# A two-layer decoder trunk on one core: the first stage's loads, products and factors reordered, and the last store moved

## The chip, the cores and the metric

The kernel runs on one core of a Trainium2 chip. Its engines each take their own list of instructions in order: TensorE (PE, with weight loads shown apart as PEld), VectorE (DVE), ScalarE (ACT), GpSimd (POOL) and SyncE (SP), which here only issues transfers. Sixteen DMA engines move the data. The metric is the device time of one execution in microseconds (us).

## The reference, cut to what matters

The input x is a matrix of 1024 rows (positions) by 1024 columns in float32. Two layers follow; each has a token mixer and a SwiGLU feed-forward network, each behind an RMS norm and added to the running sum h.

```python
def rms_norm(x, g):
    y = x * rsqrt(mean(x * x, axis=-1, keepdims=True) + 1e-6)
    return y * g

h = x
# layer 0: RG-LRU block
hn = rms_norm(h, mix_norm[0])
u = hn @ lru_w_in + lru_b_in                 # 1024 x 2048: [gate branch | recurrent branch]
rec = causal_depthwise_conv(u[:, 1024:], conv_w, conv_b)
# block-diagonal gates of rec, a linear recurrence over the rows, times gelu(gate branch), output product
h = h + rg_lru(...)
h = h + swiglu_ffn(rms_norm(h, ffn_norm[0]), ...)
# layer 1: stick-breaking attention, then an FFN again
h = h + attention(rms_norm(h, mix_norm[1]), ...)
h = h + swiglu_ffn(rms_norm(h, ffn_norm[1]), ...)
return rms_norm(h, final_norm)
```

## The kernel before

Products are made to float32 accuracy from three products of shorter numbers: each factor is cast to a high part (`whi`, `xh`) and the rest is kept as a low part (`wlo`, `xl`). One block product is then three matmuls of 128x128 by 128x512 (function `mm3`, lines 141 to 143): high by high, high weight by low x, low weight by high x. Activations stand transposed, with the model's columns on the partitions, in eight tiles `d` of 128 columns and two halves `n` of 512 rows.

The first stage (lines 251 to 360) turns x and makes the first two column tiles of the recurrent branch. It has these parts:

- `load_x(n, g)` (line 261) loads 512 rows by 256 columns of x in one transfer of 512 KB. `load_raw` (line 111) loads one weight tile of 128 columns, 512 KB, into one of three buffers `raw`. Nine small transfers (line 285) fill `vraw` with norm gains, biases and other vectors.
- `group(n, d)` (line 298): four transposes on PE (line 301) into one of four PSUM buffers `tp`; ACT scales the result into `xh` (line 304); a copy `hc` of the unscaled result is made by DVE (line 308), or by ACT (line 306) for every fourth `d`; DVE makes `xl` (line 309); and SP stores `hc` to a scratch array `hd` in DRAM (line 310), from where a later stage loads the residual. There are eight `hc` buffers, so the copies of the second half of the rows wait for the stores of the first half.
- `wsplit` (line 321) makes the two parts of a weight tile: ACT casts (line 120), POOL subtracts (line 124).
- `square_rows` (line 312) sums the squares of 128 rows on ACT; `row_factors` (line 316) makes the norm's row factors `rcol` by `rstd` (line 174): a root on ACT, then five small DVE operations with one Newton step. `broadcast_r` (line 185) spreads the factors with four small PE matmuls and a DVE copy to `rbc`.
- `project` (line 247) runs `mm3` over a range of `d` for one half of the rows; `pa[0]` and `pa[1]` are the two output tiles.

The order of the stage is written out by hand. On PE it is: the eight transposed groups of the first half, all of `project(pa[0], ..., 0)` (24 matmuls), then groups of the second half two at a time between blocks of 12 matmuls, with one transpose of `vraw` (line 345) and the two broadcasts among them. After it comes the rest of the recurrent layer; there only PE's order is by hand, and a planner places the other engines' work, partly back into the first stage. In the built program the transfer of the third weight tile (called B0 here, for the stage that uses it) stands on SP behind the store of group (1,1), and its cast on ACT stands between the squares of two row blocks of the second half, ahead of the ACT work of groups (1,6) and (1,7). Each SP transfer uses one of eight semaphores in turn, and waits until the transfer eight before it has landed.

The last stage is `finish` (line 1215): `last` makes the last products and adds them to the sum, `stats` (line 198) calls `rstd`, and `turn` (line 1235) transposes 128x512 pieces on PE and scales them by the row factor, on DVE for even row blocks and ACT for odd ones, into row-wise tiles that SP stores to `out` (line 1249). It runs in three pieces: 512 rows, 256 rows and 256 rows.

Of the kernel before, what the change touches and what calls it, by code (L numbers as in the profile page):

```python
# [8 lines left out]
F32 = mybir.dt.float32  # L9
# [7 lines left out]
P = 128  # L17
# [16 lines left out]
def trunk(  # L34
# [139 lines left out]
    def rstd(dst, ms):  # L174
        n = dst.shape[-1]
        sq = cp.tile([P, max(n, 4)], F32, tag="rs_s", name="rs_s", bufs=2)[:, 0:n]
        t = cp.tile([P, max(n, 4)], F32, tag="rs_t", name="rs_t", bufs=2)[:, 0:n]
        nc.scalar.sqrt(sq, ms)
        nc.vector.reciprocal(sq, sq)
        nc.vector.tensor_mul(t, sq, sq)  # L180
        nc.vector.tensor_mul(t, t, ms)
        nc.vector.tensor_scalar(t, t, -0.5, 1.5, op0=ALU.mult, op1=ALU.add)
        nc.vector.tensor_mul(dst, sq, t)

# [66 lines left out]
    with ExitStack() as st, tc.manual_schedule(engines={E.PE, E.Activation, E.DVE, E.Pool, E.SP}):  # L251
# [8 lines left out]

        def load_x(n, g):
            cs = slice(g * 2 * P, (g + 1) * 2 * P)
            nc.sync.dma_start(
                xt[n][:, :, cs], x[0, n * NB : (n + 1) * NB, cs].rearrange("(i p) c -> p i c", p=P)
            )

        for g in range(3):
            load_x(0, g)
        aw.append(load_raw(cols(w_in, D), (ND,)))
        load_x(0, 3)  # L270
        aw.append(load_raw(cols(w_in, D + P), (ND,)))
        load_x(1, 0)
        load_x(1, 1)
        for base, src in (
# [10 lines left out]
            nc.sync.dma_start(vraw[base : base + src.shape[0], :], src)  # L285
        load_x(1, 2)
        load_x(1, 3)
        ssum = sp.tile([P, NT], F32, name="ssum")
# [9 lines left out]
        def group(n, d):  # L298
# [5 lines left out]
            nc.scalar.activation(xh[d][n], ps, AF.Copy, scale=g)  # L304
            if d % 4 == 3:
                nc.scalar.copy(hc, ps)
            else:
                nc.vector.tensor_copy(hc, ps)
# [7 lines left out]
        def row_factors(n):  # L316
            nn = slice(4 * n, 4 * n + 4)
            nc.vector.tensor_scalar(ms[:, nn], ssum[:, nn], 1.0 / D, EPS, op0=ALU.mult, op1=ALU.add)
            rstd(rcol[:, nn], ms[:, nn])

        def wsplit(i):
            hi, lo = split(aw[i])
            aw[i] = (k3(hi), k3(lo))

        pa = [psl[0].tile([P, S], F32, tag="a", name="a_ps") for _ in range(2)]
        for d in range(6):
            group(0, d)
        wsplit(0)
        for d in (6, 7):
            group(0, d)  # L330
        wsplit(1)
        for i in range(4):
            square_rows(0, i)
        project(pa[0], aw[0], 0)
        group(1, 0)
        group(1, 1)
        row_factors(0)
        project(pa[1], aw[1], 0, range(4))
        group(1, 2)
        group(1, 3)  # L340
        project(pa[1], aw[1], 0, range(4, ND))
        group(1, 4)
        group(1, 5)
        ps = pst("vps")
        nc.tensor.transpose(ps[:, 0:P], vraw, ident)
        nc.vector.tensor_copy(vc, ps[:, 0:P])
        square_rows(1, 0)
        square_rows(1, 1)
        project(pa[0], aw[0], 1, range(4))
        group(1, 6)  # L350
        group(1, 7)
        square_rows(1, 2)
        square_rows(1, 3)
        broadcast_r(sps, "tp", 0)
        project(pa[0], aw[0], 1, range(4, ND))
        row_factors(1)
        project(pa[1], aw[1], 1, range(4))
        broadcast_r(sps, "tp", 1)
        project(pa[1], aw[1], 1, range(4, ND))

# [854 lines left out]
    def finish(h, w, R, pp, rows):  # L1215
# [19 lines left out]
        def turn(n, i0, i1, hf):  # L1235
            cs = slice(hf * NB, (hf + 1) * NB)
            for i in range(i0, i1):
# [9 lines left out]
                else:  # L1247
                    nc.vector.tensor_scalar_mul(ys[b][:, cs], ps, rcol[:, b : b + 1])
                nc.sync.dma_start(out[0, b * P : (b + 1) * P, cs], ys[b][:, cs])

        first, mid, end = (0, 0, 4), (1, 0, 2), (1, 2, 4)
        for piece in (first, mid):
# [381 lines left out]
```

## Time and profile before

| quantity | value |
|---|---|
| median of 3 runs | 2195.4 us (2195.05 to 2197.01) |
| the profiled execution | 2195.37 us |
| its span in the trace | 2193.6 us |
| PE, DVE, ACT, POOL busy | 2167.9, 1711.4, 1155.4, 315.7 us |
| first matmul of the first product | 12.39 us |
| last matmul of the first stage | about 45.5 us |
| last work on ACT and DVE | 2189.0 and 2189.2 us |

Times in the trace count from the start of the span. A row of the timeline gives the start, the duration, the engine, the source line and operation, output<-inputs, sizes, and in brackets how long the engine had been idle before it and what ended that. In the chain of waits each row is a piece of the path that ended last. SPq and ACTq are the issuing of transfers; a transfer itself takes longer, until it has landed.

### The profile page before, as it was taken

The numbers are of one execution on the slowest core, as the hardware profiler recorded it, in microseconds if no ns is written. First come the engines' busy times: TensorE is split into PE (matmuls) and PEld (weight loads), VectorE is DVE, ScalarE is ACT, GpSimd is POOL, SyncE is SP. The second block draws the span as 40 slices with busy tenths as digits, with TensorE's granted clock in tenths as the row PEclk, the third lists the DMA queues.
The fourth block names the chain that finished last, engine by engine and source line by source line (L and its number), as shares of the span: only waits on it lengthen the run. The fifth ranks groups of instructions, "written<-read, shape, count | busy, mean of one in ns | idle before, by whom it ended". The sixth has DMA issues, their size and how long they took to land.

```text
span 2193.6 us, 28494 instructions
## 1 busy us (share of the span) xinstructions
PE 2167.9 (99%) x10120; PEld 1803.3 (82%) x10120; DVE 1711.4 (78%) x2383; ACT 1155.4 (53%) x2031; POOL 315.7 (14%) x443
## 2 busy tenths in 40 slices
PE   8999999999999999999999999999999999999998
PEld 6888888888888888888888888878888888888887
DVE  6887778667777887887888888876876777788886
ACT  5567435334444544556666666753543444454556
POOL 2222020000000000004444444531000000000002
PEclk9999999999999999999999999999999999999999
DMA  7111412334444764434333333551133444467442
GB/s 232 49 48 39 135 39 64 110 125 152 141 145 138 250 221 129 148 117 104 89 106 90 94 98 105 173 169 54 48 115 116 149 146 143 144 228 236 137 153 87
DMA packets 297677, 277.71 MB, mean 127 GB/s; under 512 B 15288, under 2 KB 214080, under 8 KB 297536
## 3 DMA queue, kind: packets, MB, share of 16 engines
q1 hardware_dynamic: 297520, 275.90, 40.6%
q8 instruction: 79, 1.29, 0.2%
q14 instruction: 62, 0.51, 0.1%
q10 hardware_dynamic: 16, 0.00, 0.0%
HBM read 175.71 MB, written 74.97 MB: 114 GB/s over the span
## 4 chain that ended last, share of the span: by engine, by line
PE 95%; DVE 2%; ACT 1%; DMA 1%; SPq 0%; issue 0%; DVEq 0%; ACTq 0%
PE p_ps L143 18%; PE p_ps L141 18%; PE p_ps L142 18%; PE qk_ps L143 4%; PE qk_ps L141 4%; PE qk_ps L142 4%; PE wt_ps L1465 3%; PE ob_ps L141 2%; PE ob_ps L142 2%; PE ob_ps L143 2%; PE a_ps L141 2%; PE a_ps L142 2%; PE a_ps L143 2%; PE z_ps L1427 2%; PE z_ps L1428 2%; PE av_ps L1487 2%
## 5 line engine op out<-in xcount | busy, mean ns | idle before, releaser
L1452 POOL TENSOR_TENSOR w<-w,F 128x128 f32<-128x128 f32 (+1 forms) x192 | 192.5, 1002 | 268.3 <-DVE F L1449 164.6
L141 PE MATMUL p_ps<-vh,wch 128*128 128x512 f32 x524 | 204.2, 390 | 0.0
L143 PE MATMUL p_ps<-vh,wal 128*128 128x512 f32 x524 | 204.1, 389 | 0.1
L143 PE MATMUL p_ps<-vh,wbl 128*128 128x512 f32 x524 | 204.1, 390 | 0.0
L143 PE MATMUL p_ps<-vh,wcl 128*128 128x512 f32 x524 | 204.1, 390 | 0.0
L141 PE MATMUL p_ps<-vh,wbh 128*128 128x512 f32 x524 | 204.1, 390 | 0.0
L142 PE MATMUL p_ps<-vl,wch 128*128 128x512 f32 x524 | 203.9, 389 | 0.0
L142 PE MATMUL p_ps<-vl,wbh 128*128 128x512 f32 x524 | 203.9, 389 | 0.0
L141 PE MATMUL p_ps<-vh,wah 128*128 128x512 f32 x524 | 203.9, 389 | 0.0
L142 PE MATMUL p_ps<-vl,wah 128*128 128x512 f32 x524 | 203.8, 389 | 0.0
L668 ACT CAST wbh<-sb 128x1024 fp32r<-128x1024 f32 (+2 forms) x69 | 69.6, 1009 | 193.1 <-DVE sb L652 193.1
L1474 ACT CAST th<-wt_ps 128x512 fp32r<-128x512 f32 x192 | 92.6, 482 | 126.3 <-PE wt_ps L1465 125.8
L212 POOL TENSOR_TENSOR acc<-acc,rbc 128x512 f32<-128x512 f32 x30 | 41.6, 1386 | 771.9 <-ACT rbc L211 771.9
L1475 DVE TENSOR_TENSOR tl<-wt_ps,th 128x512 fp32r<-128x512 f32 x192 | 105.6, 550 | 48.9 <-ACT th L1474 46.9
L141 PE MATMUL qk_ps<-vh,whi 128*128 128x512 f32 x264 | 118.1, 447 | 0.0
L1449 DVE TENSOR_TENSOR_SCAN F<-F,unit 128x128 f32<-128x128 f32 (+3 forms) x128 | 115.4, 902 | 2.8 <-ACT F L1445 2.6
L143 PEld LDWEIGHTS p_ps<-vh,wbl 128*128 128x128 f32 x524 | 98.4, 188 | 21.4 <-DVE wbl L672 0.8
L143 PEld LDWEIGHTS p_ps<-vh,wal 128*128 128x128 f32 x524 | 98.3, 188 | 21.4 <-DVE wal L663 1.0
L143 PEld LDWEIGHTS p_ps<-vh,wcl 128*128 128x128 f32 x524 | 98.3, 188 | 21.1 <-DVE wcl L682 0.6
L141 PEld LDWEIGHTS p_ps<-vh,wch 128*128 128x128 f32 x524 | 98.4, 188 | 20.8 <-ACT tb L1057 0.5
L141 PEld LDWEIGHTS p_ps<-vh,wah 128*128 128x128 f32 x524 | 98.4, 188 | 20.4
L142 PEld LDWEIGHTS p_ps<-vl,wah 128*128 128x128 f32 x524 | 98.4, 188 | 20.4
(341 smaller groups left out, 5858.3 us busy)
## 6 DMA issues: line engine op xcount, KB each, us to landing
raw<-in_ffn_w_in SPq DMA_DIRECT2D x88, 512.0 KB, 4.0
vl<-pd SPq DMA_DIRECT2D x128, 256.0 KB, 3.6
pd<-U SPq DMA_DIRECT2D x90, 256.0 KB, 2.3
kk<-two SPq DMA_DIRECT2D x64, 256.0 KB, 4.2
raw<-in_ffn_w_out SPq DMA_DIRECT2D x56, 256.0 KB, 3.9
raw<-in_attn_w_qkv SPq DMA_DIRECT2D x24, 512.0 KB, 4.1
raw<-in_lru_w_in SPq DMA_DIRECT2D x16, 512.0 KB, 4.0
q<-two SPq DMA_DIRECT2D x64, 128.0 KB, 2.3
```

Source lines behind the costliest of these rows:

```text
L141: nc.tensor.matmul(ps, lhsT=wh, rhs=mh, start=first, stop=False, **kw)
L142: nc.tensor.matmul(ps, lhsT=wh, rhs=ml, start=False, stop=False, **kw)
L143: nc.tensor.matmul(ps, lhsT=wl, rhs=mh, start=False, stop=last, **kw)
L668: nc.scalar.copy(self.full(self.wb), self.full(self.sb))
L1427: nc.tensor.matmul(ps[:, 0 : c1 - c0], lhsT=lhsT, rhs=KK[q][hx][:, 0, c0:c1], start=True, stop=False)
L1428: nc.tensor.matmul(ps[:, 0 : c1 - c0], lhsT=lhsT, rhs=KK[q][hx][:, 1, c0:c1], start=False, stop=True)
L1449: nc.vector.tensor_tensor_scan(rev, rev, unit[:, NB - n :][:, ::-1], first, op0=ALU.mult, op1=ALU.add)
L1452: nc.gpsimd.tensor_mul(wt, wt, F[:, 1 : n + 1])
L1465: nc.tensor.transpose(tp[:, c : c + P], W[q, hx, j, kb // 4][:, (kb % 4) * P : (kb % 4 + 1) * P], ident)
L1474: nc.scalar.copy(th[:, q0:], tp[:, q0:])
L1475: nc.vector.tensor_sub(tl[:, q0:], tp[:, q0:], f32(th)[:, q0:])
L1487: nc.tensor.matmul(ps[:, q0:], lhsT=VV[q][:, kb, hx], rhs=tl[:, q0:], start=False, stop=last)
```

## The change

In the first stage:

- x's first two column tiles are loaded as transfers of 128 columns (256 KB) each, and the first weight tile as two halves of 256 KB, each set between pieces of x. All of x's second half of rows is loaded ahead of the nine small transfers; before, two of its four pieces came behind them.
- `hc` is copied by ACT for every odd `d` in the first half, and always by DVE in the second half.
- The two first weight tiles are split half by half (`piece`).
- On PE the first product's matmuls over `d` 0 to 3 come between the transposes of the first half: the eight that need only the high weights behind group 3, the four with the low weights behind group 5.
- The squares of the first half and their `row_factors(0)` come later, between groups of the second half; `broadcast_r(0)` and `row_factors(1)` come later too, and the last `broadcast_r` stands at the end of the stage.
- POOL copies `vraw` to `vall` before the transpose of the vectors, which moves behind four more blocks.

`rstd` has one small DVE operation less, everywhere it is used. At the end, a root of `ones` stands ahead of `finish`'s work on ACT, so that the root's table is loaded there, and the last store is issued from ACT.

In the built program the B0 transfer now stands on SP behind the store of group (1,2). Its cast on ACT stands behind group (1,5), followed by the root's table load, the root of `row_factors(0)`, and then the ACT work of groups (1,6) and (1,7). The order on all engines after the recurrent layer's first steps is the same as before, but for `rstd` and the end.

```diff
@@ rstd
         nc.vector.tensor_mul(t, sq, sq)
-        nc.vector.tensor_mul(t, t, ms)
-        nc.vector.tensor_scalar(t, t, -0.5, 1.5, op0=ALU.mult, op1=ALU.add)
-        nc.vector.tensor_mul(dst, sq, t)
+        nc.vector.scalar_tensor_tensor(t, t, -0.5, ms, op0=ALU.mult, op1=ALU.mult)
+        nc.vector.scalar_tensor_tensor(dst, t, 1.5, sq, op0=ALU.add, op1=ALU.mult)
@@ loads
-        for g in range(3):
-            load_x(0, g)
-        aw.append(load_raw(cols(w_in, D), (ND,)))
-        load_x(0, 3)
+        def load_half(raw, i):
+            src = w_in[i * NB : (i + 1) * NB, D : D + P].rearrange("(k p) c -> p k c", p=P)
+            nc.sync.dma_start(half(raw, i).rearrange("p (k c) -> p k c", k=4), src)
+
+        load_x(0, 0, 1)
+        load_x(0, 1, 2)
+        load_x(0, 2, 4)
+        aw.append(rp.tile([P, D], F32, tag="raw", name="raw"))
+        load_half(aw[0], 0)
+        load_x(0, 4, 6)
+        load_half(aw[0], 1)
+        load_x(0, 6, 8)
         aw.append(load_raw(cols(w_in, D + P), (ND,)))
-        load_x(1, 0)
-        load_x(1, 1)
+        for d in range(0, ND, 2):
+            load_x(1, d, d + 2)
...
             nc.sync.dma_start(vraw[base : base + src.shape[0], :], src)
-        load_x(1, 2)
-        load_x(1, 3)
@@ group
-            if d % 4 == 3:
+            if n == 0 and d % 2:
                 nc.scalar.copy(hc, ps)
             else:
                 nc.vector.tensor_copy(hc, ps)
@@ order of the stage
         def wsplit(i):
-            hi, lo = split(aw[i])
-            aw[i] = (k3(hi), k3(lo))
+            hi, lo = (wpool[0].tile([P, D], F32R, tag="w", name=x) for x in ("whi", "wlo"))
+            raw, aw[i] = aw[i], (k3(hi), k3(lo))
+
+            def piece(c):
+                nc.scalar.copy(half(hi, c), half(raw, c))
+                nc.gpsimd.tensor_sub(half(lo, c), half(raw, c), f32(half(hi, c)))
+
+            return piece
+
+        def pass_hi(k, first=False):
+            ps = half(pa[0], 0)
+            nc.tensor.matmul(ps, lhsT=aw[0][0][:, k], rhs=xh[k][0], start=first, stop=False)
+            nc.tensor.matmul(ps, lhsT=aw[0][0][:, k], rhs=xl[k][0], start=False, stop=False)
+
+        def pass_lo(k, last=False):
+            nc.tensor.matmul(half(pa[0], 0), lhsT=aw[0][1][:, k], rhs=xh[k][0], start=False, stop=last)
...
-        for d in range(6):
+        for d in range(4):
             group(0, d)
-        wsplit(0)
+        piece = wsplit(0)
+        piece(0)
+        for k in range(4):
+            pass_hi(k, k == 0)
+        for d in (4, 5):
+            group(0, d)
+        piece(1)
+        for k in range(4):
+            pass_lo(k)
         for d in (6, 7):
             group(0, d)
-        wsplit(1)
-        for i in range(4):
-            square_rows(0, i)
-        project(pa[0], aw[0], 0)
+        piece = wsplit(1)
+        piece(0)
+        piece(1)
+        for k in range(4, ND):
+            pass_hi(k)
+        for k in range(4, ND):
+            pass_lo(k, k == ND - 1)
         group(1, 0)
         group(1, 1)
-        row_factors(0)
         project(pa[1], aw[1], 0, range(4))
+        square_rows(0, 0)
+        square_rows(0, 1)
         group(1, 2)
         group(1, 3)
+        square_rows(0, 2)
+        square_rows(0, 3)
         project(pa[1], aw[1], 0, range(4, ND))
         group(1, 4)
         group(1, 5)
-        ps = pst("vps")
-        nc.tensor.transpose(ps[:, 0:P], vraw, ident)
-        nc.vector.tensor_copy(vc, ps[:, 0:P])
-        square_rows(1, 0)
-        square_rows(1, 1)
+        row_factors(0)
         project(pa[0], aw[0], 1, range(4))
         group(1, 6)
         group(1, 7)
-        square_rows(1, 2)
-        square_rows(1, 3)
+        for i in range(4):
+            square_rows(1, i)
+        project(pa[0], aw[0], 1, range(4, ND))
         broadcast_r(sps, "tp", 0)
-        project(pa[0], aw[0], 1, range(4, ND))
+        project(pa[1], aw[1], 1, range(4))
+
+        vall = sp.tile([P, P], F32, name="vall")
+        nc.gpsimd.tensor_copy(vall, vraw)
+        ps = pst("vps")
+        nc.tensor.transpose(ps[:, 0:P], vall, ident)
+        nc.vector.tensor_copy(vc, ps[:, 0:P])
         row_factors(1)
-        project(pa[1], aw[1], 1, range(4))
+        project(pa[1], aw[1], 1, range(4, ND))
         broadcast_r(sps, "tp", 1)
-        project(pa[1], aw[1], 1, range(4, ND))
@@ finish
-                nc.sync.dma_start(out[0, b * P : (b + 1) * P, cs], ys[b][:, cs])
+                queue = nc.scalar if (n, i, hf) == (1, 3, 1) else nc.sync
+                queue.dma_start(out[0, b * P : (b + 1) * P, cs], ys[b][:, cs])
...
+        nc.scalar.sqrt(rcol[:, 0:1], ones)
         first, mid, end = (0, 0, 4), (1, 0, 2), (1, 2, 4)
```

More of the change, by code (lines that the diff above doesn't have):

```diff
@@ L259, in trunk, with load_x @@
         aw = []
-        def load_x(n, g):
-            cs = slice(g * 2 * P, (g + 1) * 2 * P)
+        def load_x(n, d0, d1):
+            cs = slice(d0 * P, d1 * P)
             nc.sync.dma_start(
```

## The prediction

> **What bounds the kernel now.** I read the busy shares first, then who waited for whom on PE, then the chain of waits in the first 60 us and in the last 20, then each engine's timeline there.
>
> ```profile
> PE 2167.9 (99%) x10120; PEld 1803.3 (82%) x10120; DVE 1711.4 (78%) x2383; ACT 1155.4 (53%) x2031; POOL 315.7 (14%) x443
> ```
>
> PE is idle for 2193.6 - 2167.9 = 25.7 us of the span, so a change that adds or drops no product can gain only there. The waits of PE in the first 90 us:
>
> ```profile
> PE tp L301 <- DMA xt<-in_x: 3.3, 2, 1.9
> ...
> PE rb_ps L189 <- DVE rcol L183: 1.8, 1, 1.8
> PE a_ps L143 <- POOL wlo L124: 1.3, 1, 1.3
> ...
> PE a_ps L142 <- DVE xl L309: 0.6, 1, 0.6
> ```
>
> The diff addresses each of these. Taken one by one they suggest some 7 us (with 1.0 in front of the transpose `vps`, below). The chain says something else:
>
> ```profile
> 17.90 5.50 DMA hd<-hc
> ...
> 26.18 5.60 DMA raw<-in_lru_w_in
> 31.80 1.05 ACT whi L120
> ...
> 39.05 2.12 DVE rs_t L180
> 41.86 1.16 PE rb_ps L189 x8
> 43.02 0.23 PE a_ps L141
> ...
> 45.75 0.23 PE a_ps L141
> ```
>
> The stage ends at 45.75 (12 matmuls of 0.227 behind 43.02). What decides that is a path through SP: the first store of a residual piece, its landing (which frees the `hc` buffer for the second half of the rows), then the load of the third weight tile B0 behind two such stores, and its cast on ACT, behind which ACT makes the last tiles of x. PE's waits before 17 us don't lie on it.
>
> **The change part by part.** *Early pieces and passes.*
>
> ```profile
> 4.39 3.68 PE L301 MATMUL tp<-ident,xt 128*128 128x128 f32 x16 [1.88 <-DMA xt<-in_x]
> 11.56 1.07 PE L301 MATMUL tp<-ident,xt 128*128 128x128 f32 x8 [1.37 <-DMA xt<-in_x]
> 19.49 1.03 PE L301 MATMUL tp<-ident,xt 128*128 128x128 f32 x8
> 8.11 0.69 ACT L304 ACTIVATE xh<-tp,g 128x512 fp32r<-128x512 f32 x1 [0.17 <-PE tp L301]
> 8.70 0.58 ACT L306 COPY hc<-tp 128x512 f32<-128x512 f32 x1
> ```
>
> A first piece of half the size should let PE start up to 0.8 us before 4.39, but the four groups it now makes first still end near 8.0, since their last two need the same first megabyte of x as now. PE then has the first products ahead of it in its queue. They need the cast half tile, and ACT has four `xh` and now two copies first: the fourth `xh` starts near 8.1 to 8.4, the copy behind it ends near 9.4, the half cast (half of 1.05) near 10.0. So PE idles some 2 us where it transposed before. From 10.0 it has 24 matmuls (5.4) and 16 transposes (2.1), plus about 1.5 while it still runs at the slow rate of the early rows (0.23 a transpose against 0.13 later): 19.0, against 19.49 now. Half a microsecond, and it is covered anyway: the next thing DVE waits for is a store.
>
> *Moved loads.* On SP two loads of x now come ahead of the nine small ones.
>
> ```profile
> 14.71 0.31 SPq L285 DMA_DIRECT2D vraw<-in_lru_gate_b  x1
> 16.18 0.28 SPq L285 DMA_DIRECT2D vraw<-in_lru_lambda  x1
> ...
> 16.84 0.95 SPq L263 DMA_DIRECT2D xt<-in_x  x2
> 17.90 8.23 SPq L310 DMA_DIRECT2D hd<-hc  x10
> 23.52 0.69 DVE L308 COPY hc<-tp 128x512 f32<-128x512 f32 x1 [8.30 <-DMA hd<-hc]
> 24.78 0.68 DVE L308 COPY hc<-tp 128x512 f32<-128x512 f32 x1
> ```
>
> The step of 1.47 us is SP waiting for a 512 KB load to land, one per small transfer (a semaphore is used again eight transfers later). With two more loads ahead, the wait at 16.18 ends at 16.18 + 2 x 1.47 = 19.1; the first store follows after what is now 17.90 - 16.18 less the 0.95 of the two loads: 19.9, two microseconds later. But nothing is queued in front of it, where before it landed 5.50 after issue behind two loads. Bounds of its landing:
>
> ```profile
> DMA to landing us min/median/max: 3.6/5.5/7.1
> DMA to landing us min/median/max: 2.1/2.4/2.8
> DMA to landing us min/median/max: 3.8/5.7/7.6
> ```
>
> These are the residual stores, the output stores and the first weight loads. Between 2.1 and 3.6 I take 3.0, nearer the residual stores: landed at 22.9, so DVE resumes 0.5 us sooner than 23.52. Per group DVE takes 1.26 us (23.52 to 24.78). All copies of the second half are DVE's now, and the B0 load stands behind the third store, not the second: issue at 26.18 - 0.5 + 1.26 = 26.9. PE reaches group (1,2) at 19.0 + 1.03 + 12 x 0.227 = 22.8 and its `xh` is made by 24.2; DVE wants it at 25.4, so PE is 1.2 us early and is not the bound here.
>
> B0 lands 3.8 (the shortest) to 5.6 (as before) after issue: 30.7 to 32.5. Eleven stores stand ahead of it instead of ten stores and two loads, but they start 2 us later; I take 4.8, so 31.7, as good as unchanged.
>
> *Factors later.* ACT's order behind that cast is new: table load, root, then the last two `xh`.
>
> ```profile
> 21.41 1.28 ACT L178 ACT_TABLE_LOAD   x1
> 26.88 0.16 DVE L181 TENSOR_TENSOR rs_t<-rs_t,ms 128x4 f32<-128x4 f32 x1
> 27.08 0.17 DVE L182 TENSOR_SCALAR rs_t<-rs_t 128x4 f32<-128x4 f32 x1
> 28.81 0.30 PE L345 MATMUL vps<-ident,vraw 128*128 128x128 f32 x1 [1.04 <-issue]
> 36.48 0.39 PE L141 MATMUL a_ps<-xh,whi 128*128 128x512 f32 x1
> ```
>
> The table load was in ACT's idle time at 21.41; now it cannot start before the cast is done. Cast 31.7 to 32.75, table 34.05, root (0.2) 34.25; DVE's four small operations at steps of 0.20 to 35.1 (the queued ones stand ahead of the last two groups); two groups of DVE, 2.6, to 37.7; PE's last two matmuls of `pa[0]` end at 38.2. Before, the last tile's three matmuls begin at 36.48 and end at 37.17, so this point moves 1.0 later. What PE had left by then (22.8 + 1.03 + 2.72 + 1.03 + 2.72 + 1.03 + 6 x 0.227 = 32.7) it has done, and it waits.
>
> Behind 38.2 follow broadcast (half of 1.16), 12 matmuls, the transpose of vectors (0.30; its wait for many transfers has gone to POOL), 12 matmuls, broadcast: 0.58 + 2.72 + 0.30 + 2.72 + 0.58 = 6.9, so 45.1. The wait of 1.8 for `rcol` is gone: the second factors are ready near 43.3, since DVE does them behind the transpose of vectors, and PE wants them at 44.5. Gain of the stage: 45.75 - 45.1 = **0.65 us**, from +1.65 (B0 at 30.7) to -0.15 (at 32.5), and 0.8 less if DVE's small operation again takes 2.12 beside POOL as at 39.05. The next stage's DVE work starts some 2 us later, but PE has two stages of 24 x 2 matmuls (21.8) before it needs it.
>
> *The end.* The chain there, and the timelines:
>
> ```profile
> 2174.66 1.80 PE e_ps L1244 x16
> 2176.46 0.12 PE o_ps L141
> ...
> 2177.89 0.45 PE e_ps L1244 x4
> ```
> ```profile
> 2175.52 0.16 DVE L203 TENSOR_SCALAR ms<-st_ps 128x4 f32<-128x4 f32 x1
> 2175.71 1.28 ACT L178 ACT_TABLE_LOAD   x1
> 2177.00 0.21 ACT L178 ACTIVATE rs_s<-ms 128x4 f32<-128x4 f32 x1
> 2178.32 1.41 DVE L1248 TENSOR_SCALAR y<-e_ps,rcol 128x512 f32<-128x512 f32 x2
> 2182.21 0.41 DVE L1230 TENSOR_TENSOR hh<-o_ps,hh 128x256 f32<-128x256 f32 x1
> 2188.95 1.41 SPq L1249 DMA_DIRECT2D out<-U  x3
> ```
>
> The table now loads where ACT idles ahead of `finish`, so the root starts at 2175.71 (-1.29), and one small operation less gives -0.20: scaling starts at 2176.83. Then PE becomes the bound: products until 2177.89, 16 transposes (1.80), 12 matmuls (1.43), so the add now at 2182.21 can start at 2181.25, 0.96 sooner. The two roots behind it save 0.20 each: **1.36 us**; all of 1.29 + 0.60 = 1.89 if PE does not bind, 0.9 if it is later still. Three issues take 1.41 on SP; the last no longer queues behind the others: **0.4 us**, between 0 and 0.47.
>
> The Trainium skill's "ScalarE: Activation LUTs", section "What ACT_TABLE_LOAD costs", counts a drain of about 1.38 us beside the load's 1.28, so by it hiding the load would gain 2.7 and the sum be 1.4 lower, 2191.6. The trace shows the load and no drain (root 0.01 behind it); I go by the trace.
>
> Other uses of `rstd` lie beside PE's products (PE waits for none of them): 0.
>
> Sum: -0.65 - 1.36 - 0.4 = -2.4 us. The profiled execution took 2195.37, its span 2193.6; the median is 2195.4, the same. So 2193.0, span 2191.2. What a measurement tells from no change, 0.2%, is 4.4 us: bounds 2191.0 and 2199.8.
>
> **The rivals.** *PE falls back to its slow rate.* Between 32.7 and 38.2 PE runs six matmuls and waits the rest, 2 us at a stretch. The early rows show a rate not much over half the later one, on work of the same kind. If it comes back, the 6.9 us behind 38.2 grow by up to 6.9; for half of them 3.4: 2193.0 + 3.4 = 2196.4, slower than before. It decides from 2.4 us on, 11 matmuls at half rate. Against it: the idle 1.8 before 41.86 is followed by steps of 0.23. The skill's "TensorE: Matmul & The Clock Gate" (Part 1: the HAM clock gate) says that PE halves its clock after an idle window of about 3.4 us and needs a busy one to recover. No run here shows a return to the slow rate, and my longest single wait is below that.
>
> *B0 is no bound.* If the queue is emptier than I think, B0 lands at 30.7 and the first store at 22.0, which pulls B0 another 0.9: the stage gains 2.55, all 4.3: 2191.1. With the end's 1.89 as well 2190.6. For it: 2 us later stores leave the queue a gap near 20; against it: three of the four landings above are 3.6 or longer.
>
> *The end gains little*: PE's last products bind fully, or the store's issue on ACT saves nothing: 1.0 less or so, 2194.1.
>
> **Chances.** Forecast 55% (2191.8 to 2193.9), little gain at the end 11% (2193.9 to 2195), slow PE 18% (2194.5 to 2200.5, 8 of it over 2199.8), B0 no bound 16% (2189.5 to 2191.8, 14 of it below 2191.0). So faster 14%, same 78%, slower 8%. Range 2190.2 to 2196.8.
>
> **What would show it.** Right: first store issued near 20 and DVE resuming near 23; B0 issued near 26.9; ACT with cast, table, root in a row near 32 to 34; no PE wait for `rcol`; the next stage starting near 45; the root at the end without a table load ahead of it. Wrong: transposes or matmuls at the slow rate behind 33; B0 landing before 30 or behind 33; the last add starting behind 2181.3 counted from the old end.

## The result and the profile after

The changed kernel takes 2199.1 us (median of 22 executions, 2197.2 to 2201.0), the kernel before 2195.6 us beside it (22, 2194.8 to 2197.5). The ratio is 1.0015, with a 95% interval of 1.0009 to 1.0021: slower by 0.15%, where 2193.0 us and a gain were forecast. The profiled execution took 2200.57 us, its span 2198.7 us, so it lies 1.5 us above the median; a second profile stands among the experiments.

The timeline of PE in the changed kernel (start, duration, line, operation; in brackets the idle time before it and what ended it):

```profile
11.25 0.80 PE L341 MATMUL a_ps<-xh,whi 128*128 128x512 f32 x1 [1.77 <-ACT whi L334]
...
14.84 1.91 PE L308 MATMUL tp<-ident,xt 128*128 128x128 f32 x8
...
22.42 1.03 PE L308 MATMUL tp<-ident,xt 128*128 128x128 f32 x8
...
37.40 0.49 PE L141 MATMUL a_ps<-xh,whi 128*128 128x512 f32 x1 [1.66 <-ACT xh L311]
39.41 0.50 PE L142 MATMUL a_ps<-xl,whi 128*128 128x512 f32 x1 [1.52 <-DVE xl L316]
...
40.67 0.80 PE L142 MATMUL a_ps<-xl,whi 128*128 128x512 f32 x1 [0.29 <-DVE xl L316]
...
41.69 1.91 PE L188 MATMUL rb_ps<-ident,rcol 128*128 128x128 f32 x8
...
49.24 1.05 PE L188 MATMUL rb_ps<-ident,rcol 128*128 128x128 f32 x8
51.28 0.50 PE L141 MATMUL a_ps<-xh,whi 128*128 128x512 f32 x1 [0.99 <-DVE rbc L195]
```

The row at 22.42 is group (1,0), the first of the second half of the rows: before, it stood at 19.49. The last row is the first product of the next stage. In the timeline of before that product starts here:

```profile
45.59 0.39 PE L141 MATMUL a_ps<-xh,whi 128*128 128x512 f32 x1
```

So the first stage is longer by 51.28 - 45.59 = 5.7 us in this execution. (The prediction's 45.75 is the same product in the chain of waits, which dates pipelined products a little later.) Nothing behind it gives that back: the first product of the last stage's output tile is later still, by 6.7.

SP, DVE and ACT in the same timeline of the changed kernel:

```profile
20.62 7.83 SPq L317 DMA_DIRECT2D hd<-hc  x11
28.50 0.43 SPq L114 DMA_DIRECT2D raw<-in_lru_w_in  x1
...
23.78 0.69 DVE L315 COPY hc<-tp 128x512 f32<-128x512 f32 x1 [2.68 <-ACT xh L311]
...
27.42 0.69 DVE L315 COPY hc<-tp 128x512 f32<-128x512 f32 x1 [1.03 <-ACT xh L311]
...
37.02 0.69 DVE L180 TENSOR_TENSOR rs_t<-rs_s 128x4 f32<-128x4 f32 x1
...
34.20 1.05 ACT L120 CAST whi<-raw 128x1024 fp32r<-128x1024 f32 x1 [2.61 <-DMA raw<-in_lru_w_in]
35.27 1.28 ACT L178 ACT_TABLE_LOAD   x1
36.56 0.21 ACT L178 ACTIVATE rs_s<-ms 128x4 f32<-128x4 f32 x1
36.68 1.25 ACT L311 ACTIVATE xh<-tp,g 128x512 fp32r<-128x512 f32 x2
```

DVE takes up the second half at 23.78, and what it waited for is no longer the store but ACT's `xh`, that is PE's late transposes. It waits for `xh` again until 27.42, for group (1,2), behind whose store B0 stands. B0 is asked for at 28.50 (26.18 before) and has landed at 34.20 (31.80 before). Behind its cast stand the table load and the root, and only then the last two `xh`, for which PE waits at 37.40. I call these three ahead of the last `xh` the pile.

PE by stretches, with the granted clock in the column behind the count of matmuls. First the kernel before, then the changed kernel:

```profile
35.00:45.00 10.00, 7.54 (x37) 1.00 0.67 216
```
```profile
35.00:45.00 10.00, 6.53 (x24) 0.83 0.63 199
```

The slow rate came back: from 40.67 to the next matmul's start it takes 0.59 us and from there 0.43, instead of 0.23, and the broadcast at 41.69 takes 1.91 instead of the 1.05 of the one at 49.24. Near 43.9 the steps are short again.

The end of the changed kernel (DVE, SP, ACT):

```profile
2182.20 0.15 DVE L202 TENSOR_SCALAR ms<-st_ps 128x4 f32<-128x4 f32 x1
...
2183.50 0.75 DVE L1286 TENSOR_SCALAR y<-e_ps,rcol 128x512 f32<-128x512 f32 x1
...
2187.77 0.42 DVE L1268 TENSOR_TENSOR hh<-o_ps,hh 128x256 f32<-128x256 f32 x1 [0.31 <-PE o_ps L143]
...
2192.91 1.41 DVE L1286 TENSOR_SCALAR U<-e_ps,rcol 128x512 f32<-128x512 f32 x2
...
2192.40 2.62 SPq L1289 DMA_DIRECT2D out<-U  x4
...
2194.19 0.38 ACTq L1289 DMA_DIRECT2D out<-U  x1
```

From the mean squares to the first scaling it takes 1.30 us, where it took 2.80 (2175.52 to 2178.32). That is the end's gain.

### The profile page after: what moved, and what is told of

Its sections match the earlier page's. It is cut to its first block, busy times and chain, and to the rows that moved or that the text cites. A ratio compares the mean times of both kernels' runs of the same rounds, so it can differ in the third digit from the quotient of the medians.

```text
span 2198.7 us, 28495 instructions
## 1 busy us (share of the span) xinstructions
PE 2172.5 (99%) x10120; PEld 1805.7 (82%) x10120; DVE 1708.0 (78%) x2374; ACT 1156.0 (53%) x2034; POOL 315.0 (14%) x446
## 4 chain that ended last, share of the span: by engine, by line
PE 95%; DVE 3%; ACT 1%; DMA 1%; issue 0%; SPq 0%; DVEq 0%; ACTq 0%
PE p_ps L143 18%; PE p_ps L141 18%; PE p_ps L142 18%; PE qk_ps L143 4%; PE qk_ps L141 4%; PE qk_ps L142 4%; PE wt_ps L1507 3%; PE ob_ps L142 2%; PE ob_ps L141 2%; PE ob_ps L143 2%; PE a_ps L142 2%; PE a_ps L141 2%; PE a_ps L143 2%; PE z_ps L1469 2%; PE z_ps L1470 2%; PE av_ps L1529 2%
## 5 line engine op out<-in xcount | busy, mean ns | idle before, releaser
L142 PEld LDWEIGHTS p_ps<-vl,wbh 128*128 128x128 f32 x524 | 98.4, 188 | 20.5
```

What stands on the lines that cost most here:

```text
L142: nc.tensor.matmul(ps, lhsT=wh, rhs=ml, start=False, stop=False, **kw)
```

## The experiments

The theory at the start: PE falls behind in the early passes, so SP asks for B0 late, and the pile (B0's cast, the table load and the root on ACT) then holds up the last `xh`; PE waits, falls back to the slow rate, and the broadcast at the very end adds a wait. Rivals: the passes themselves cost the time; the moved loads do; the slow rate alone does. "Next stage" below is the start of the first product of the third tile: 45.6 before, 51.28 in the changed kernel. The kernel before was timed beside each group of runs, at 2195.8 to 2195.9.

**end_only.** The kernel before with the three edits of the end (`rstd` in two operations, the root ahead of `finish`, the last store from ACT).

```diff
-        nc.vector.tensor_mul(t, t, ms)
-        nc.vector.tensor_scalar(t, t, -0.5, 1.5, op0=ALU.mult, op1=ALU.add)
-        nc.vector.tensor_mul(dst, sq, t)
+        nc.vector.scalar_tensor_tensor(t, t, -0.5, ms, op0=ALU.mult, op1=ALU.mult)
+        nc.vector.scalar_tensor_tensor(dst, t, 1.5, sq, op0=ALU.add, op1=ALU.mult)
...
+                queue = nc.scalar if (n, i, hf) == (1, 3, 1) else nc.sync
...
+        nc.scalar.sqrt(rcol[:, 0:1], ones)
```

> The kernel before with the three edits of the end alone (root table loaded ahead of the last products, the normalisation factor in two operations for three, last store issued on ACT). Theory: the first stage is untouched, so the next stage starts at 45.6 to 45.8 us as before, and the end gains what the changed kernel's profile shows there, about 1.5 us: 2194.0 against 2195.5. Rival (the end gains nothing and what the changed kernel lost is less than its first stage shows): 2195.5. Rival (the last store gains the 0.4 of the prediction as well): 2193.6.

Measured 2193.76 us, ratio 0.9990 (0.9981 to 0.9999). The end gains; against this kernel, whose next stage starts at 45.05, the changed kernel loses 5.3 us by the medians; in the profiled executions it is 7.1, of which 6.2 by the start of the next stage.

**end_no_store.** The same with the last store back on SP.

> The run end_only (2193.8) with the last store back on SP, so that only the table and the shorter factor are changed at the end. Theory (the landing of the last store, not its issue, ends the run): from the start of the last scaling to the end of the span it takes 5.8 us as with the store on ACT, and the time is within 0.2 of end_only. Rival (the prediction's step): 0.4 us more, 2194.2.

Measured 2194.11, 0.35 more than end_only, where the theory had 0.2 at most and the rival 0.4. The last scaling (timeline) and the span (view of the cores), end_only first, then end_no_store:

```profile
core 0 of [0], span 2191.7 us
```
```profile
2185.77 1.41 DVE L1247 TENSOR_SCALAR U<-e_ps,rcol 128x512 f32<-128x512 f32 x2
```
```profile
core 0 of [0], span 2192.7 us
```
```profile
2186.85 1.41 DVE L1247 TENSOR_SCALAR U<-e_ps,rcol 128x512 f32<-128x512 f32 x2
```

From there to the end of the span it takes 5.9 us with the store on ACT and 5.8 without: the move of the store gains nothing there. The 1.0 by which the spans differ lies ahead of the last scaling, and the executions of the two (2193.3 to 2195.4 and 2193.4 to 2195.1) overlap, so the 0.35 doesn't speak for the rival.

**early_b0.** The changed kernel, with B0 loaded ahead of the stores:

```diff
             nc.sync.dma_start(vraw[base : base + src.shape[0], :], src)
+        b0 = [load_raw(cols(w_in, 0), (ND,))]
```

> The changed kernel with one load moved: the third weight tile (B0) is asked for on SP right behind the nine small loads, ahead of the residual stores, so its cast on ACT no longer stands between the first squares and the root late in the stage. Theory (the late cast, the table load and the root in a row hold back the last xh, PE waits for them and falls to the slow rate): PE's waits for xh and xl behind 35 us go, the slow rate does not come back, and the next stage starts near 45.5 us where it started at 51.28: 2193.3. Rival (the passes and the slow first products cost the time, whatever B0 does): the next stage still starts behind 49 us and the time is above 2197.

Measured 2195.50, 3.6 us less than the changed kernel. PE's timeline:

```profile
35.90 0.50 PE L142 MATMUL a_ps<-xl,whi 128*128 128x512 f32 x1 [0.41 <-DVE xl L317]
...
37.15 0.50 PE L142 MATMUL a_ps<-xl,whi 128*128 128x512 f32 x1 [0.29 <-DVE xl L317]
...
46.27 0.50 PE L141 MATMUL a_ps<-xh,whi 128*128 128x512 f32 x1 [0.99 <-DVE rbc L195]
```

The long waits and the slow rate are gone, with the passes untouched. The size was overstated: the wait for the broadcast's copy (0.99) stays, which I had left out of the expected 45.5, and the profile I started from was 1.5 above the median. Against end_only, whose end it shares, 1.7 us are still missing.

**early_table.** The changed kernel, one line: `nc.scalar.sqrt(rcol[:, 0:1], ones)` as ACT's first operation.

> The changed kernel with one small root as ACT's first operation, so that the first table loaded is the one that the factors need too, and no table load stands before the root of the first factors. B0's load stays where it is. Theory (cast, table load and root in a row ahead of the last xh are the cost): the last two xh no longer wait behind the table load, PE's waits of 1.66 and 1.52 us go or fall below 0.5, next stage at 46 to 47.5: 2195.3 to 2196.5. Rival (B0's late landing is the cost, the table load only an addition): 1.3 us less, next stage near 50, 2197.8.

Measured 2195.28, next stage at 45.99. Without the table load the planner also put B0's cast behind the last `xh`, so the whole pile is gone, not the table load alone: the run doesn't tell the two apart. early_b0 does in part: there the table load (31.43) and the root (33.58) still stand ahead of the last `xh` (33.69), in time that ACT had to spare, and the loss of 3.6 us went with B0's cast alone.

**np_b0.** early_b0 with the passes undone (groups 0 to 7, then `project(pa[0], aw[0], 0)`).

```diff
-        for d in range(4):
+        for d in range(6):
             group(0, d)
...
-        for k in range(4):
-            pass_hi(k, k == 0)
-        for d in (4, 5):
-            group(0, d)
...
-        for k in range(4, ND):
-            pass_lo(k, k == ND - 1)
+        project(pa[0], aw[0], 0)
```

> The run early_b0 (B0 asked for early, 2195.5, next stage at 46.27) with the early passes undone as well: all eight groups of the first half of the rows, then its products. Theory (the passes only cost while B0's chain hangs on the second half's groups): group (1,0) is transposed near 19.5 where it was at 22, but the first residual store sets the second half's pace again, so the next stage starts at 45.3 to 46.3: 2194.5 to 2195.5. Rival (the passes themselves cost some 2.5 us on PE): next stage near 43.7, 2193.0.

Measured 2196.53, next stage at 46.91: a microsecond worse than with the passes, where neither theory had it. DVE's timeline:

```profile
25.83 0.69 DVE L316 COPY hc<-tp 128x512 f32<-128x512 f32 x1 [9.38 <-DMA hd<-hc]
```

Group (1,0) came at 20.05, so PE was early enough, but the first store now landed 2.3 us later than before (23.52), behind the moved loads and B0. In early_b0 DVE waits for that store too, until 25.46, so this pair doesn't price the passes by themselves. But undoing them gains nothing here, and early_b0 got rid of most of the loss with them in place: the rival that the passes are the loss falls.

**loads_back.** The changed kernel with `load_x(1, 4, 6)` and `load_x(1, 6, 8)` behind the nine small transfers again.

> The changed kernel with the last two loads of x back behind the nine small ones, as before. Theory (the loads that moved cost SP two microseconds that nobody waits for in the changed kernel, since PE and ACT are later still): first residual store asked for near 18, B0 still asked for behind the store of group (1,2) near 28, the time at 2199.1 within 0.7. Rival (the moved loads delay B0 and so make the loss): B0 asked for near 26, 2197 or less.

Measured 2200.67 (2198.7 to 2201.8), next stage at 50.25. The first store was asked for at 18.67 and B0 at 27.92, and the pile and the slow rate stayed. The time is 1.6 us above the changed kernel's, outside the 0.7 that I expected, for a reason that I didn't find; it isn't a gain, so the moved loads are not the loss.

**dummy.** The changed kernel with 12 matmuls of no use around the seventh tile's first product.

```diff
+        def idle(c):
+            for _ in range(c):
+                nc.tensor.matmul(half(pa[1], 1), lhsT=aw[1][0][:, 0], rhs=xh[0][0], start=True, stop=True)
+        project(pa[0], aw[0], 1, range(4, 6))
+        idle(6)
...
+        idle(6)
```

> The changed kernel with 12 products of no use (into a half of PSUM that is overwritten later) where PE waited for the last xh and xl (6 ahead of the seventh tile's first product, 6 behind it). It computes the same result. Theory (PE's idle time of 1.66 and 1.52 us brought the slow rate back from 40.67 to 43.8 us): the steps stay at 0.23 us, and the next stage starts about 1.2 us sooner, 50.1: 2197.9. Rival (the slow rate is not tied to those waits): steps of 0.43 us again near 41 us, and the time the same, 2199.1, or up to 0.3 longer if the added products delay the needed ones.

**bc_mid.** The changed kernel with `broadcast_r(sps, "tp", 1)` six products earlier.

```diff
-        project(pa[1], aw[1], 1, range(4, ND))
+        project(pa[1], aw[1], 1, range(4, 6))
         broadcast_r(sps, "tp", 1)
+        project(pa[1], aw[1], 1, range(6, ND))
```

> The changed kernel with the second broadcast put between the last 12 products (behind 6 of them) where it stood behind all. Theory: only the wait of the next stage for the copy of the broadcast out of its PSUM (0.99 us before the product at 51.28) goes, as six products (1.4 us) run beside that copy: next stage near 50.3, 2198.1. Rival (PE then waits for the second factors at the broadcast, which came ready just before): no gain, 2199.1.

Measured 2198.87 and 2198.76: neither differs from the changed kernel by more than the runs scatter. PE by stretches, dummy first, then bc_mid; below them two rows of bc_mid's timeline:

```profile
35.00:45.00 10.00, 9.71 (x47) 1.00 0.63 197
```
```profile
35.00:45.00 10.00, 7.85 (x24) 0.66 0.53 159
```
```profile
37.64 0.80 PE L142 MATMUL a_ps<-xl,whi 128*128 128x512 f32 x1 [1.51 <-DVE xl L316]
...
47.31 1.13 PE L188 MATMUL rb_ps<-ident,rcol 128*128 128x128 f32 x8 [0.20 <-DVE cb L438]
```

Two more rows of bc_mid, PE and SP:

```profile
20.27 1.04 PE L308 MATMUL tp<-ident,xt 128*128 128x128 f32 x8
...
26.85 0.55 SPq L114 DMA_DIRECT2D raw<-in_lru_w_in  x1
```

With PE kept busy the clock stays at 1.00 in dummy's profile; without, it falls to 0.66 in bc_mid, by twice as much as in the changed kernel. So it is the gaps that bring the slow rate. In dummy's profile the next stage starts at 49.29, and from the start of B0's cast to there it takes 16.0 us, against 17.1 and 17.3 in the two profiles of the changed kernel: by that the slow rate is worth 1.1 to 1.3 us. The median of dummy doesn't confirm it: its executions scatter over 4.8 us, and B0's cast starts anywhere from 32.44 to 34.20 in these profiles. In bc_mid the broadcast's wait is gone and the longer slow stretch takes its place.

bc_mid also shows that PE's lateness is not needed for the loss. Its order is that of the changed kernel up to the last products, but in its profiled execution group (1,0) came at 20.27 for 22.42, and B0 was asked for at 26.85, as I had forecast (26.9). The next stage still began at 49.68 only: PE waited 2.05 and 1.51 us for the last `xh` and `xl`, and the slow rate did the rest.

**factors_back.** The changed kernel with the first factors where they were before:

```diff
+        for i in range(4):
+            square_rows(0, i)
         for k in range(4, ND):
             pass_hi(k)
...
         group(1, 1)
+        row_factors(0)
```

> The changed kernel with the first factors where the kernel before has them: squares of the first half behind its last casts, the factors behind group (1,1), so table load and root come before group (1,2) and not behind B0's cast. Passes, pieces, loads and the late broadcast stay. Theory (the pile of cast, table load and root ahead of the last xh is the loss; the passes alone are not): no wait of PE for the last xh above 0.7, no slow rate behind 35 us, next stage at 46 to 47: 2195.3 to 2196.3. Rival (the late second half through passes and slow products is the loss, wherever the factors are): next stage behind 49, 2198 or more.

Measured 2199.27: no gain. The timeline of POOL, DVE and PE says why:

```profile
45.13 2.34 POOL L124 TENSOR_TENSOR wlo<-rawg,whi 128x1024 fp32r<-128x1024 f32 x1 [2.71 <-ACT whi L120]
...
45.20 2.29 DVE L413 TENSOR_SCALAR pq<-gq 128x8 f32<-128x8 f32 x1
...
48.08 0.67 DVE L195 COPY rbc<-rb_ps 128x512 f32<-128x512 f32 x1
...
48.81 0.80 PE L141 MATMUL a_ps<-xh,whi 128*128 128x512 f32 x1 [3.77 <-DVE rbc L195]
```

The pile was gone and PE through with its last broadcast at 45.0 (48.81 less 3.77). But a DVE operation of eight elements a row ran for as long as POOL's subtraction beside it, the copy of the broadcast stood on DVE behind it, and the next stage's first product needs the PSUM space that this copy frees. PE idled 3.77 us and started at the slow rate. A second cost, hidden behind the first.

**factors_back_bc.** factors_back with the broadcast of bc_mid.

> The run factors_back (2199.3) with the second broadcast between the last products too (6 behind it). factors_back had no wait for the last xh left, PE ended its last broadcast near 44.9, and then waited 3.77 us for the copy of the broadcast, which stood on DVE behind an operation of 8 elements a row that took 2.29 us (45.20) beside POOL's subtraction (45.13), and fell to the slow rate. Theory (two costs, the pile ahead of the last xh and the broadcast at the very end, each large enough for the whole loss): with both gone the next stage starts at 45 to 46.2, 2194.3 to 2195.6. Rival (the passes and moved loads cost by themselves): 2197 or more.

Measured 2195.43, next stage at 46.19. With both costs gone the time is that of the kernel before again, with passes, pieces and moved loads still in this kernel. It is not all of the loss: end_only, with the same end, is 1.7 us faster.

**after_again.** The changed kernel once more.

> The changed kernel once more for a second profile, since the first one (2200.6) lies 1.5 us above its median (2199.1). Theory: the same places lose (last xh behind cast, table load and root; the broadcast's copy), and what varies between executions is when B0 lands and whether and for how long the slow rate comes back: next stage at 49 to 51.3.

One time, 2200.1. Next stage at 50.37; waits of 0.79, 1.54 and 0.30 for the last `xh` and `xl`, 0.99 for the broadcast's copy, clock 0.83 between 35 and 45. The places are the same.

**What the stage before waits for.** old_b0_vall: the kernel before with the end's edits, B0 ahead of the stores, and the copy `vall` on POOL.

```diff
         load_x(1, 3)
+        b0 = [load_raw(cols(w_in, 0), (ND,))]
...
+        nc.gpsimd.tensor_copy(vall, vraw)
...
-        nc.tensor.transpose(ps[:, 0:P], vraw, ident)
+        nc.tensor.transpose(ps[:, 0:P], vall, ident)
```

> The kernel before with the three edits of the end and two of the first stage: B0 asked for on SP ahead of the residual stores, and the small vectors copied by POOL ahead of their transpose. Passes, pieces, factors and load order as before. Theory (B0's cast on ACT and PE's waits behind it set the stage's end, with the wait of 1.04 us before the transpose of vectors and 1.8 us for the second factors): the next stage starts at 42 to 43.5 where it started at 45.75, 2190.3 to 2191.8. Rival (the first residual store, which frees the buffer that DVE waits for at 23.5, sets the pace whatever B0 does): next stage at 45 or later, 2193.2 or more.

Measured 2196.79, 3 us worse than end_only. DVE and PE in the timeline, then PE by stretches:

```profile
25.63 0.69 DVE L308 COPY hc<-tp 128x512 f32<-128x512 f32 x1 [10.23 <-DMA hd<-hc]
...
30.85 0.30 PE L347 MATMUL vps<-ident,vall 128*128 128x128 f32 x1 [1.83 <-DVE xl L309]
```
```profile
27.00:35.00 8.00, 5.41 (x20) 0.79 0.80 293
```

B0 ahead of the first store makes that store land 2.1 us later, DVE waits for it, PE for DVE, and the slow rate comes back here too. So the first store does set DVE's pace. The run doesn't take B0's bound away alone, since it delays the store.

hc16_end and hc16_vall_end: end_only with 16 buffers `hc` for 8, and the same with `vall`.

```diff
-            hc = sp.tile([P, NB], F32, tag="hc", name="hc", bufs=8)
+            hc = sp.tile([P, NB], F32, tag="hc", name="hc", bufs=16)
```

> The kernel before with the edits of the end and 16 buffers instead of 8 for the residual pieces, so that no copy of the second half waits for a store to land. Theory (in the stage before the change, the landing of the first residual store sets DVE's pace and through it PE's and SP's): DVE's wait of 8.3 us until 23.5 goes, DVE takes up the second half near 20.5, SP asks for B0 near 23 instead of 26.2, and the next stage starts at 43 to 44: 2190.8 to 2192.2. Rival (B0's load and the factors set the end, the store is covered): next stage at 45 or later, 2193.2 or more.

> The run hc16_end with the small vectors copied by POOL ahead of their transpose, as in the changed kernel. Theory: the wait of 1.0 us that PE has before the transpose of vectors goes, and with PE no longer late for other reasons the whole of it is gained, unless the second factors are then waited for: next stage 0.3 to 1.0 sooner than in hc16_end, 2190.0 to 2191.9. Rival (the factors are the bound): as hc16_end.

Measured 2193.93 and 2194.52: no gain over end_only. SP, ACT and DVE of hc16_end:

```profile
25.74 0.46 SPq L114 DMA_DIRECT2D raw<-in_lru_w_in  x1
...
31.48 1.05 ACT L120 CAST whi<-raw 128x1024 fp32r<-128x1024 f32 x1 [2.19 <-DMA raw<-in_lru_w_in]
...
20.45 0.69 DVE L307 COPY hc<-tp 128x512 f32<-128x512 f32 x1 [5.15 <-ACT xh L303]
```

DVE is 3 us earlier, but SP still takes 8.3 us over ten stores (8.23 before), though their copies are made earlier, so B0 is asked for when it was, and its cast lies where it lay. Two bounds stand side by side; how far apart they are is not shown.

best_b takes both away: end_only with 16 buffers, `vall`, and B0 behind the first two loads of the second half.

```diff
         load_x(1, 1)
+        b0 = [load_raw(cols(w_in, 0), (ND,))]
```

> The kernel before with the end's edits, 16 buffers for the residual pieces, the copy of the small vectors on POOL, and B0 asked for behind the first two loads of the second half. Theory (two bounds lie side by side in the stage before the change, the first store and B0's cast, so that old_b0_vall, which took away the second alone, and hc16_vall_end, which took away the first alone, gained nothing): with both gone the next stage starts at 41.5 to 43.5, 2189.8 to 2191.8. Rival (a third bound, the second factors, is as late): next stage at 44.5 or later, 2192.8 or more.

Measured 2192.65 (2191.5 to 2193.2), ratio 0.9985 (0.9976 to 0.9993): faster than both kernels. ACT and PE:

```profile
17.37 1.05 ACT L120 CAST whi<-raw 128x1024 fp32r<-128x1024 f32 x1 [1.97 <-DMA raw<-in_lru_w_in]
...
39.00 1.16 PE L188 MATMUL rb_ps<-ident,rcol 128*128 128x128 f32 x8 [1.11 <-DVE rcol L182]
...
42.73 0.41 PE L141 MATMUL a_ps<-xh,whi 128*128 128x512 f32 x1
```

The next stage starts at 42.73, as expected; the median lies 0.85 above the range, the profiled execution (2191.5) in it. The second factors are waited for next.

after_hc16 and after_fix: the changed kernel with 16 buffers, and with early_b0, bc_mid and 16 buffers together.

> The changed kernel with 16 buffers for the residual pieces. Theory (in the changed kernel PE comes to the second half so late that the store has long landed; cast, table and root hold back the last xh): the stores of the second half keep their times, B0 is asked for at the same place, and the time stays at 2199.1, within 0.6. Rival (the first store, asked for 2.7 us later since the moved loads, is what the changed kernel waits for): 2 us or more gained, 2197 or less.

> The changed kernel with three repairs: B0 asked for early (as in early_b0), the second broadcast between the last products (as in bc_mid), 16 buffers for the residual pieces. Theory: from early_b0 (2195.5, next stage at 46.27) the broadcast gains the 1.0 us of its wait, the buffers nothing or little: next stage at 45.0 to 45.4, 2194.3 to 2194.8, so the pieces and passes gain nothing over the kernel before with its end changed (2193.8). Rival (the early passes are worth something once nothing else holds the stage): 2193 or less.

Measured 2200.33 (2198.0 to 2202.0) and 2195.40. The buffers are of no use there, as the theory has it, though the first is 0.6 above its range. after_fix is no better than early_b0: with the broadcast earlier, PE waits for the second factors instead, and the next stage starts at 46.49. Nothing that I tried on the changed first stage brought it below the 45.6 of before; 45.99 in early_table came nearest.

## Why the prediction was wrong

The steps that failed are three terms of the sum: the point 38.2, at which PE is through with `pa[0]` (it was 41.7), the 6.9 us behind it (8.6), and a wait for the copy of the last broadcast, which had no term (1.0). The chain of B0, cast, table load and root was right in kind. Point by point, by the prediction's own steps:

- *"19.0, against 19.49 now"*, for the time when PE is through with the first half. It was 22.42 in the profiled execution, the first number that failed. The cast came a good microsecond later than the 10.0 that I took (x's next piece let PE go on at 7.5 only), and then I charged "about 1.5 while it still runs at the slow rate". PE ran slow until 16.3: eight products at 0.43 instead of 0.23, and eight transposes in 1.91 instead of 1.03, from 11.25 on; and at 20.49 it waited 0.55 us for `xl`. I had kept the slow rate's end nearly where it was. That the idle time of the passes prolongs the slow start is not shown: np_b0, without the passes, ran slow until 15.3, and bc_mid, with them, only until 13.2.
- *"PE is 1.2 us early and is not the bound here."* It was the bound: DVE waits for `xh` until 23.78, and again until 27.42 in front of the store that B0 follows. The store of the first piece, asked for at 20.62 (forecast 19.9), mattered no longer.
- *"issue at 26.9"* and *"I take 4.8, so 31.7"* for B0: 28.50, and 5.7 to its landing at 34.2. Issue follows from the step above; the flight was 0.1 longer than the upper of my bounds. bc_mid, with the issue at 26.85, lost as well, so this step alone does not make the loss.
- *Cast, table, root in a row, then the last tiles*: right in kind. PE's two last matmuls of `pa[0]` ended at 41.7 for 38.2: 2.5 of it is B0's, 0.5 the small DVE operation at 37.02, which took 0.69 beside POOL (I had named that risk, at 0.8, and left it out of the sum), and 0.5 the slow rate of these two matmuls.
- *6.9 us behind that point*: 8.6, from 41.69 to 50.29. The slow rate is some 1.1 of the 1.7 (the first broadcast and two products). Most of the rest is a row that I misread: "half of 1.16" for a broadcast, where the row is one whole broadcast. The slow rate is the rival that PE falls back, which I gave 18%; it came, but with the 0.5 above it is only some 1.5 of the loss.
- *The broadcast at the end.* I counted its 0.58 on PE and no wait behind it. The next stage's first product waits for the copy out of its PSUM: 0.99 us from the end of the broadcast here, 3.77 in factors_back. The prediction had no such step.

Together 3.5 + 1.7 + 1.0 = 6.2 us, from the forecast 45.1 to 51.28. At the median the loss is smaller: 3.5 us net, with 1.5 (the trace) to 2.1 (end_only) gained at the end. The opening sum is off too, though nothing hangs on it: PE's four waits are 7.0 us without the 1.0 in front of `vps`, 8.0 with it.

- *The end, 1.36*: 1.5, right. The first scaling comes 1.50 sooner, PE takes 0.38 of it back at 2187.77 (forecast 0.53), and the two later roots give 0.40. A drain beside the table load, for which the Trainium skill ("ScalarE: Activation LUTs", section "What ACT_TABLE_LOAD costs") would have 1.4 us more, does not show here either.
- *The last store, 0.4*: 0 to 0.1 by the traces of end_only and end_no_store.
- *B0 decides the stage before*: half right. With the first store's bound away (hc16_end) SP's own pace asks for B0 no sooner, and only best_b, with both away, gains; the chain of waits shows one of the two.

What is shown: B0's late cast in front of the last `xh` costs most of the loss (early_b0 takes 3.6 of 5.3 us off, with the passes in place), the broadcast at the end is a second cost, and the passes, pieces and moved loads bring no gain when both are mended. Not settled: how the pile's cost divides between waiting and the slow rate (dummy), and the 1.7 us by which the mended kernels stay behind end_only; the next stage starts 1.2 later in early_b0 than there.

Between the first stage and the last the changed kernel loses another 1.0 us (6.7 less 5.7). Some 0.6 of it has to do with the edits of the end, not with the first stage, as end_only and early_b0 lose it at the same place. DVE and PE of the changed kernel show it:

```profile
2155.91 1.65 DVE L690 TENSOR_TENSOR sb<-raw 128x384 f32<-128x384 f32 x1
...
2161.73 0.50 PE L143 MATMUL p_ps<-vh,wbl 128*128 128x512 f32 x1 [0.23 <-DVE wbl L710]
```

Beside it an operation of POOL takes 1.75 us (from 2155.40). In the kernel before, POOL's takes 2.81 and this one of DVE 0.56, and PE doesn't wait. What decides which of the two gives way is not shown.

## What to carry to other kernels

Work that is moved "later, where the engine is idle" lands in front of something: ask for each engine's queue what the moved operation now delays, and what frees the memory that the next stage starts with. A path that the chain of waits shows may have a twin that is little shorter; take both away together before judging either. And idle gaps on PE may cost twice, as here, where the slow rate followed them.

## What the runs showed of the hardware

**The slow rate comes back after broken-up waits.** In the changed kernel it came after gaps of 1.66, 1.52 and 0.29 us, with four matmuls among them, and in its second profile after 0.79, 1.54 and 0.30. If the slow clock is half the full one (the steps are 0.43 for 0.23), a granted clock of 0.83 over 10 us is an estimated 0.17 x 10 / 0.5 = 3.4 us at the slow rate; 0.66 in bc_mid gives 6.8, twice that. The single wait of 1.8 us in the kernel before did not do it. It doesn't hang on the order alone: in end_only the clock is 0.90 over the first 17 us, where the kernel before, with the same order there, has 1.00. The Trainium skill ("TensorE: Matmul & The Clock Gate", Part 1) has free-running windows of about 3.4 us, which agrees with both stretches; its rule of no idle gaps of more than about 3.4 us (section "HAM oscillation — how this bites in real kernels") would have let these kernels pass, as the longest of these gaps is 1.66 us in the changed kernel and 2.05 in bc_mid.

**The slow start does not show as a granted clock.** In the changed kernel the products from 11.25 to 14.41 follow each other at 0.43, and the view by stretches gives:

```profile
0.00:17.00 17.00, 10.19 (x35) 1.00 0.94 281
```

So the clock column tells of a return (0.83 above), not of the beginning; there the steps of the matmuls have to be read.

**A tiny DVE operation can take as long as POOL's.** 2.29 us for 128x8 at 45.20 in factors_back, beside POOL's 2.34 from 45.13; the prediction's row at 39.05 (2.12 for 128x4) is of the same kind, and so is the 0.69 for 128x4 at 37.02 in the changed kernel, beside POOL's 2.35 from 35.33. Each ends within 0.05 us of POOL's operation. The Trainium skill ("SBUF — State Buffer", section "SBUF: two separate sides") has it that the two engines share a port pair which one of them holds for a whole instruction, and these rows agree.
